# RMSNorm and SiLU over 8192 rows: loads five blocks ahead instead of four, and gamma's row on the ScalarE queue

## The chip, the cores and the metric

The kernel runs on one core of a Trainium2 chip. The metric is the device time of one execution in microseconds; smaller is better. Of the engines, it uses VectorE (DVE in the profile), ScalarE (ACT), GpSimd (POOL) and SyncE (SP). The data is moved by 16 DMA engines, which work off what SyncE, and in the changed kernel also ScalarE, issues. TensorE does nothing here.

## The reference

The input x has 8 x 1024 rows of 2048 float32 numbers; gamma has 2048 numbers, and eps is 1e-5. Each row is divided by its root mean square, multiplied by gamma and put through SiLU:

```python
rms = np.sqrt(np.mean(x ** 2, axis=-1, keepdims=True) + eps)
out = gamma * x / rms
return (out * (1 / (1 + np.exp(-out)))).astype(np.float32)
```

The input is 67 MB and so is the output. Each number is read once and written once.

## The kernel before

The 8192 rows are cut into 16 blocks (`nblk`) of 512 rows. A block is one tile of 128 partitions, and each partition holds four whole rows (`J = 4`), that is 4 x 2048 numbers or 32 KB. So a block is 4 MB, and one DMA loads it and one stores it. The tiles come from a pool of six buffers (`BUFS`), used in turn. All work on a block is done in place: the load writes the tile, VectorE and ScalarE overwrite it, and the store reads it. The buffer is free again when its store has landed.

The order of the instructions on each engine is the order in which the code is written (`manual_schedule`); the framework only adds the waits. `load(b)` (line 49) issues the load on SyncE. `stats(b)` sums the squares of the four rows: ScalarE does three of them (line 63), VectorE one (line 59), and GpSimd makes 1/rms out of the sums with a multiply-add (line 66) and a power (line 69). `finish(b)` multiplies each row by its 1/rms and by gamma on VectorE (line 74), applies SiLU on ScalarE to pairs of rows (line 78), and issues the store on SyncE (line 79).

Before the loop, gamma's row is fetched into the first partition of a tile of the same pool (line 84; it takes one of the six buffers for a while), the first `LEAD` loads are issued, and GpSimd copies gamma from that partition to all 128 (line 89) into a tile of its own. In the loop, step b does `stats(b + 1)`, then `finish(b)`, then `load(b + LEAD)`. So SyncE's queue holds, after the first loads, store 0, load 4, store 1, load 5 and so on. SyncE takes one instruction after the other: an instruction that waits holds up all those behind it.

With six buffers, of which gamma's row has the first, block k uses buffer (k + 1) mod 6. With `LEAD = 4`, load b + 4 is written where block b - 2 was, and waits for store b - 2. In the queue it stands directly behind store b.

Of the kernel before, what the change touches and what calls it, by code (L numbers as in the profile page):

```python
# [1 line left out]

# [4 lines left out]

ACT = mybir.ActivationFunctionType
ALU = mybir.AluOpType


@with_exitstack
def kernel(
    ctx: ExitStack,
    tc: tile.TileContext,
    x: bass.AP,
    gamma: bass.AP,
    eps: bass.AP,
    out: bass.AP,
):  # L20

    nc = tc.nc
    P = nc.NUM_PARTITIONS
    f32 = mybir.dt.float32
    x2 = x.flatten_outer_dims()
    o2 = out.flatten_outer_dims()
    n, d = x2.shape
    J = 4  # L30
    BUFS, LEAD = 6, 4
    nblk = n // (P * J)
    xb = x2.rearrange("(b p j) d -> b p (j d)", p=P, j=J)
    ob = o2.rearrange("(b p j) d -> b p (j d)", p=P, j=J)

    singles = ctx.enter_context(tc.tile_pool(name="singles", bufs=1))
    pool = ctx.enter_context(tc.tile_pool(name="pool", bufs=BUFS))
    small = ctx.enter_context(tc.tile_pool(name="small", bufs=4))
    psum = ctx.enter_context(tc.tile_pool(name="psum", bufs=1, space=bass.MemoryType.PSUM))

    g = singles.tile([P, d], f32)
    half = singles.tile([P, J], f32)
    junk_a = psum.tile([P, d], f32, name="junk_a")
    junk_v = psum.tile([P, d], f32, name="junk_v")
    blocks, rstds = {}, {}

    def load(b):
        xt = pool.tile([P, J * d], f32, name="xt")
        nc.sync.dma_start(out=xt, in_=xb[b])  # L49
        blocks[b] = xt  # L50

    def row(b, j):
        return blocks[b][:, j * d:(j + 1) * d]

    def stats(b):
        ss = small.tile([P, J], f32, name="ss")
        for j in range(J):
            if j == J - 1:
                nc.vector.tensor_tensor_reduce(  # L59
                    out=junk_v, in0=row(b, j), in1=row(b, j), scale=1.0, scalar=0.0,  # L60
                    op0=ALU.mult, op1=ALU.add, accum_out=ss[:, j:j + 1])
            else:
                nc.scalar.activation(out=junk_a, in_=row(b, j), func=ACT.Square,  # L63
                                     accum_out=ss[:, j:j + 1])
        var = small.tile([P, J], f32, name="var")
        nc.gpsimd.tensor_scalar(out=var, in0=ss, scalar1=1.0 / d, scalar2=float(eps),  # L66
                                op0=ALU.mult, op1=ALU.add)
        rstd = small.tile([P, J], f32, name="rstd")
        nc.gpsimd.tensor_tensor(out=rstd, in0=var, in1=half, op=ALU.pow)  # L69
        rstds[b] = rstd  # L70

    def finish(b):
        for j in range(J):
            nc.vector.scalar_tensor_tensor(out=row(b, j), in0=row(b, j), scalar=rstds[b][:, j:j + 1],  # L74
                                           in1=g, op0=ALU.mult, op1=ALU.mult)
            if j % 2:
                pair = blocks[b][:, (j - 1) * d:(j + 1) * d]
                nc.scalar.activation(out=pair, in_=pair, func=ACT.Silu)  # L78
        nc.sync.dma_start(out=ob[b], in_=blocks.pop(b))  # L79
        del rstds[b]  # L80

    with tc.manual_schedule():
        grow = pool.tile([P, J * d], f32, name="xt")
        nc.sync.dma_start(out=grow[0:1, 0:d],  # L84
                          in_=bass.AP(tensor=gamma.tensor, offset=gamma.offset, ap=[[d, 1], gamma.ap[0]]))
        for b in range(LEAD):
            load(b)
        nc.gpsimd.memset(half, -0.5)  # L88
        nc.gpsimd.partition_broadcast(g, grow[0:1, 0:d])  # L89
        stats(0)  # L90
        for b in range(nblk):
            if b + 1 < nblk:
                stats(b + 1)
            finish(b)
            if b + LEAD < nblk:
                load(b + LEAD)


# [1 line left out]
_INS = ['x', 'gamma', 'eps']  # L100
_OUTS = [((8, 1024, 2048), 'float32')]

_NUMBERS = {'eps': 9.999999747378752e-06}


# [26 lines left out]
```

## Time and profile before

| | |
|---|---|
| median of 13 runs | 322.48 us (321.2 to 323.99) |
| the profiled execution: its own time | 322.32 us |
| the profiled execution: span from first to last instruction | 320.5 us |
| VectorE busy | 181.7 us (57%) |
| ScalarE busy | 213.7 us (67%) |
| GpSimd busy | 59.5 us (19%) |
| moved by DMA | 134.24 MB, mean 419 GB/s |
| busy share of SyncE's DMA queue | 97.9% of the span of 16 DMA engines |

The span runs from the first to the last instruction of the core; the time around it (322.32 - 320.5 = 1.8 us) is launch and end. An engine's busy time counts its compute instructions. The DMA figures are means over 16 DMA engines, which means that one of them can be late without the mean showing it. Where the profile names SPq, it means SyncE's queue, in which the DMAs are issued; the time to landing runs from an issue to the moment at which all parts of the transfer have been reported.

### The profile page before, as it was taken

How to read it: one execution, taken by the hardware profiler on the slowest of the kernel's cores; microseconds unless marked ns; L12 is line 12 of the kernel's file. 1: busy time of each engine (PE TensorE's matmuls, PEld its weight loads, DVE VectorE, ACT ScalarE, POOL GpSimd, SP SyncE). 2: the span in 40 equal slices, each digit the busy share in tenths (PEclk: the TensorE clock that was granted, in tenths of full speed). 3: DMA queues.
4: the chain of work that ended last, by engine and by line, in shares of the span. 5: the costliest groups of instructions: out<-in, count | busy, mean ns of one | idle time of the engine just before them, and what ended most of it. 6: DMA issues, size and time to landing. Idle time of an engine off the chain costs nothing.

```text
span 320.5 us, 432 instructions
## 1 busy us (share of the span) xinstructions
DVE 181.7 (57%) x96; ACT 213.7 (67%) x130; POOL 59.5 (19%) x38
## 2 busy tenths in 40 slices
DVE  0209998485490934909358192762917639099500
ACT  1349999988474874748657486773857848487800
POOL 0212232213040220402104031040400404012000
DMA  8999999999999999999999999999999999997994
GB/s 316 405 442 417 433 429 413 388 446 433 425 450 409 443 438 397 458 433 414 450 417 433 450 409 450 438 413 438 425 433 446 417 438 438 425 446 331 446 429 192
DMA packets 4612, 134.24 MB, mean 419 GB/s; under 512 B 513, under 2 KB 513, under 8 KB 513
## 3 DMA queue, kind: packets, MB, share of 16 engines
q1 hardware_dynamic: 4610, 134.23, 97.9%
q14 instruction: 2, 0.02, 0.0%
HBM read 67.12 MB, written 67.11 MB: 419 GB/s over the span
## 4 chain that ended last, share of the span: by engine, by line
DMA 60%; DVE 17%; ACT 13%; issue 5%; DVEq 1%; SPq 1%; ACTq 0%
DMA xt<-in_x_dram 60%; DVE xt L74 16%; ACT xt L78 8%; ACT junk_a L63 4%; DVEq L127 1%; SPq L79 0%; DVE ss L59 0%; DVE junk_v L59 0%; SPq L49 0%; SPq L84 0%; DVEq L59 0%; ACTq L63 0%; DVEq L74 0%
## 5 line engine op out<-in xcount | busy, mean ns | idle before, releaser
L74 DVE SCALAR_TENSOR_TENSOR xt<-xt,rstd,g 128x2048 f32<-128x2048 f32 x64 | 146.1, 2346 | 1.1 <-POOL rstd L69 1.1
L63 ACT ACTIVATE junk_a<-xt 128x2048 f32<-128x2048 f32 x48 | 90.3, 1880 | 67.4 <-DMA xt<-in_x_dram 66.4
L78 ACT ACTIVATE xt<-xt 128x4096 f32<-128x4096 f32 x32 | 115.5, 3615 | 23.0 <-DVE xt L74 23.0
L59 DVE CUSTOM_DVE_ANT_0 junk_v<-xt 128x2048 f32<-128x2048 f32 x16 | 36.8, 2299 | 118.4 <-DMA xt<-in_x_dram 118.4
L66 POOL TENSOR_SCALAR var<-ss 128x4 f32<-128x4 f32 x16 | 15.0, 935 | 221.3 <-ACT junk_a L63 209.5
L69 POOL TENSOR_TENSOR rstd<-var,half 128x4 f32<-128x4 f32 x16 | 42.0, 2624 | 1.3
L63 ACT ACTIVATION_READ_ACCUMULATOR junk_a<-xt 128x1 f32 x48 | 8.9, 186 | 0.0
L89 POOL PARTITION_BROADCAST g<-xt x1 | 2.3, 2304 | 8.0 <-issue 8.0
L59 DVE DVE_READ_ACCUMULATOR2_ANT ss<- 128x1 f32 x16 | 2.3, 141 | 0.0
L63 ACT ACT_TABLE_LOAD x1 | 1.3, 1283 | 0.7 <-PEq L113 0.7
L78 ACT ACT_TABLE_LOAD x1 | 1.3, 1283 | 0.0
L88 POOL MEMSET half<- 128x4 f32 x1 | 0.1, 102 | 0.3 <-POOLq L113 0.3
L113 POOL MEMSET const-float32-0.0<- 128x1 f32 x1 | 0.1, 99 | 0.2 <-issue 0.2
L113 POOL MEMSET const-bfloat16-1.0<- 128x1 bf16 x1 | 0.1, 102 | 0.0
L113 POOL MEMSET const-uint8-127<- 128x1 uint8 x1 | 0.1, 102 | 0.0
L113 POOL MEMSET const-float32-1.0<- 128x1 f32 x1 | 0.1, 99 | 0.0
## 6 DMA issues: line engine op xcount, KB each, us to landing
xt<-in_x_dram SPq DMA_DIRECT2D x16, 4096.0 KB, 42.6
out_dram<-xt SPq DMA_DIRECT2D x16, 4096.0 KB, 33.3
xt<-in_gamma_dram SPq DMA_DIRECT2D x1, 8.0 KB
```

What stands on the lines that cost most here:

```text
L59: nc.vector.tensor_tensor_reduce(out=junk_v, in0=row(b, j), in1=row(b, j), scale=1.0, scalar=0.0, op0=ALU.mult, op1=ALU.add, accum_out=ss[ ...
L63: nc.scalar.activation(out=junk_a, in_=row(b, j), func=ACT.Square, accum_out=ss[:, j:j + 1])
L66: nc.gpsimd.tensor_scalar(out=var, in0=ss, scalar1=1.0 / d, scalar2=float(eps), op0=ALU.mult, op1=ALU.add)
L69: nc.gpsimd.tensor_tensor(out=rstd, in0=var, in1=half, op=ALU.pow)
L74: nc.vector.scalar_tensor_tensor(out=row(b, j), in0=row(b, j), scalar=rstds[b][:, j:j + 1], in1=g, op0=ALU.mult, op1=ALU.mult)
L78: nc.scalar.activation(out=pair, in_=pair, func=ACT.Silu)
L88: nc.gpsimd.memset(half, -0.5)
L89: nc.gpsimd.partition_broadcast(g, grow[0:1, 0:d])
L113: nc = _bacc.Bacc("TRN2", target_bir_lowering=False, num_devices=1)
L127: with _tile.TileContext(nc) as tc:
```

## The change

Two edits. `LEAD` goes from 4 to 5, so five loads are issued before the loop, and in the loop load b + 5 stands behind store b. The number of buffers stays at six. And gamma's row is fetched by a DMA that ScalarE issues, ahead of all its other work, instead of by the first DMA in SyncE's queue.

```diff
-    BUFS, LEAD = 6, 4
+    BUFS, LEAD = 6, 5
...
     with tc.manual_schedule():
         grow = pool.tile([P, J * d], f32, name="xt")
-        nc.sync.dma_start(out=grow[0:1, 0:d],
-                          in_=bass.AP(tensor=gamma.tensor, offset=gamma.offset, ap=[[d, 1], gamma.ap[0]]))
+        nc.scalar.dma_start(out=grow[0:1, 0:d],
+                            in_=bass.AP(tensor=gamma.tensor, offset=gamma.offset, ap=[[d, 1], gamma.ap[0]]))
         for b in range(LEAD):
             load(b)
```

With this, load b + 5 is written where block b - 1 was, and waits for store b - 1. On SyncE, 16 loads and 16 stores remain; the last five stores stand behind all loads, where there were four.

## The prediction

> **What bounds the kernel now.** I read the page's first three parts first: engines, the row of DMA digits, the queues.
>
> ```profile
> span 320.5 us, 432 instructions
> ...
> DVE 181.7 (57%) x96; ACT 213.7 (67%) x130; POOL 59.5 (19%) x38
> ...
> DMA  8999999999999999999999999999999999997994
> ...
> q1 hardware_dynamic: 4610, 134.23, 97.9%
> ```
>
> No compute engine is busy above 67%; the one DMA queue moves 134.23 MB and is busy 97.9% of the span, 9 tenths or more in nearly every slice. Only the first slice and the last four dip. So time can only come from those edges or from a change in how fast the 16 DMA engines work. A busy share is a mean over 16, so next I ask whether the queue ever runs short: SyncE's issues in order of time, and the two lines' times from issue to landing.
>
> ```profile
> 39.27 0.35 SPq L79 DMA_DIRECT2D out_dram<-xt  x1
> 39.66 0.43 SPq L49 DMA_DIRECT2D xt<-in_x_dram  x1
> ...
> 139.30 0.34 SPq L79 DMA_DIRECT2D out_dram<-xt  x1
> 139.70 0.58 SPq L49 DMA_DIRECT2D xt<-in_x_dram  x1
> ...
> 257.06 48.11 SPq L79 DMA_DIRECT2D out_dram<-xt  x4
> ```
>
> ```profile
> DMA to landing us min/median/max: 13.9/33.3/35.1
> ```
>
> That last line is of the stores (L79); the loads (L49) have:
>
> ```profile
> DMA to landing us min/median/max: 12.2/42.6/43.6
> ```
>
> Each load goes out 0.4 us behind its store and never waits. A 4.19 MB transfer needs about 9.7 us (below), so a store landing after 33.3 us found some 33.3 - 9.7 = 24 us of work queued ahead of it. The queue isn't short in the middle. The tail is where it looks short; here are windows of 1 us (the last two columns are the DMA share and GB/s):
>
> ```profile
> 293.00:294.00 1.00, 1.00 (x1) 1.00 (x1) 0.00 (x0) 1.00 0.83 360
> 294.00:295.00 1.00, 1.00 (x2) 1.00 (x1) 0.00 (x0) 1.00 0.31 131
> 295.00:296.00 1.00, 1.00 (x1) 0.76 (x1) 0.00 (x0) 1.00 0.30 131
> 296.00:297.00 1.00, 1.00 (x2) 0.33 (x1) 0.00 (x0) 1.00 1.22 524
> ```
>
> (A packet counts where it falls, so shares over 1 occur.) For two microseconds only about a third of the engines have work: store 13 is through on the others and store 14 isn't issued before ScalarE ends its Silu at 295.77 (292.15 + 3.62). It is tempting to book these 2 us as the gain of an earlier last load. So I went to the trace's landing marks, sixteen for every transfer, one per DMA engine. First and last mark: store 12 284.70 and 290.30, store 13 294.38 and 299.99, store 14 306.75 and 309.68, store 15 316.45 and 319.32. The last marks are 9.69, 9.69 and 9.64 apart, as they are over most of the run (9.69 from the median of all transfers), while the first jump by 12.37 between stores 13 and 14. The engines that idle are the ones that lead by 5.6 us; the laggards never stop, and **the laggards end the run**. Their whole path is a sum: 13.35 (last mark of load 0) + 31 x 9.69 = 313.7, + 5.6 of extra time in seven transfers = 319.3, then 1.2 to the span's end. The extras: load 1 1.06, load 3 1.00, load 4 1.06, store 3 0.34, load 7 0.63, store 5 0.80, load 12 0.70.
>
> **What the Trainium skill says.** "DMA: Bandwidth & Descriptors", Queues, rings and completion order: each DMA engine takes descriptors in order from its own ring and round-robins between queue rows at packet borders. Every engine thus runs at its own pace, as the marks show; a gamma row on the second queue need not sit behind the loads. Same page, Why a DMA increments its semaphore by 16 and not by 1: a transfer over 128 partitions uses 16 engines and is complete only when all have reported. The trace agrees: 513 packets under 512 B are 32 x 16 + 1, so gamma's is on one engine. So a load that waits for a store waits for the laggard. Same page, Issuing engines are not separate DMA queues: another issuer saves only issue time. The trace of before has nothing on ScalarE's queue.
>
> **The change, part by part.**
>
> 1. *Gamma's issue leaves SyncE.* Load 0's issue moves from 1.12 to 0.72 us, when gamma's began: 0.40. First load packets started at 2.10, so now at about 1.7 if descriptor generation doesn't collide with ScalarE's. Bounds: 0 to 0.40; I take 0.40. Gamma's 8 KB packet (0.31 us) stays on one engine in both kernels. ScalarE issues it at 0.72 and its table load (1.28 us) slips by 0.35, covered by ScalarE's wait for load 0, which lasts to 13.37. The broadcast of gamma began at 8.85, though gamma had landed at 2.5; that is 6 us of cover, and its result is first read at 26.46, against a broadcast end of 11.15: 15 us more.
>
> 2. *A fifth load up front.* Its issue is another 0.45 us on SyncE (four took 1.90), at about 2.6 us, with SyncE idle until 39.27. Store 0 now has five loads ahead of it: its slot is the sixth instead of the fifth, so it starts at about 52 instead of 42. It is issued at 39.27 either way (ScalarE sets that), 13 us early. Load 5 takes gamma's old buffer, free since 11.15, so it goes out at 39.66 unhindered.
>
> 3. *A new wait.* With six buffers, load b+5 writes where block b-1 was, so it waits for store b-1 to land on all engines; before, load b+4 waited for store b-2. In the new queue order store b-1, load b+4, store b, load b+5, store b+1, the wait ends with load b+4 and store b still queued: 2 x 9.7 = 19.4 us for the laggard, 19.4 - 5.6 = 13.8 us for a leading engine. From SyncE's issue to the first packet took 1.0 us (1.12 to 2.10), the issue itself 0.6. So the wait costs the DMA nothing. Ten loads (6 to 15) wait, each most of a 19.4 us round. Behind each on SyncE stands store b+1. It is ready early: it needs load b+2, which landed three slots (29 us) before, and the compute from a load's landing to the store ahead of it is about 15 us (load 15 lands at 280.62, store 14 goes out at 295.77). Nobody but the load into its buffer waits for that store, and it too has two transfers ahead.
>
> 4. *The tail.* Load 15 moves from slot 28 to 27, 9.7 us earlier, store 15 goes out near 304.8 - 9.7 - 0.7 = 294.4 and its turn comes at about 303.5 at the earliest engine. The leaders' idle goes: their median mark steps by 12.19 from store 13 to 14, 2.5 us too much, and ten of sixteen marks do so. Price: nothing, by the marks above, since the laggards have all 32 transfers back to back anyway. Upper bound if idle engines could pass on their share of the rate: 10 x 2.5 / 16 = 1.6 us.
>
> 5. *One turn fewer.* The queue changes from a load to a store 12 times instead of 13. Four of the thirteen loads ahead of a store (3, 4, 7, 12) took extra, 3.4 us together, 0.26 a turn. I don't know that the turn is the cause (load 1 has no store near it), so bounds are 0 and 1.06; I take 0.26.
>
> Sum: 0.40 + 0 + 0 + 0 + 0.26, so 0.7 us. The profiled execution took 322.32 with span 320.5; I expect a span of 319.8 and 321.6 for it, and from the median of 322.48, which lies 0.16 above the profiled one, **321.8 us**.
>
> **Rivals.** *The tail pays after all* (faster). If the rate is shared, so that engines with nothing to do leave bandwidth to others, the 1.6 us of part 4 come back, and with part 1 it is 322.48 - 2.0 = 320.5. For it: the dip in the windows. Against it: 32 KB packets take 1213 ns nearly always in the trace, and the laggards' 9.69 didn't shorten while the others idled. In the same case I count the extras: should most of those 5.6 us be due to stores issued close to a turn, the new order, which issues 19 us ahead, may drop 1 to 3 us of them.
>
> *Turns get dearer* (slower). The first two turns (loads 3 and 4) cost 1.0 each, later ones 0 to 0.7; the first loads had been issued in a bunch, far ahead of their turn. In the new order every store is issued some 29 us ahead of its own, and if that makes turns cost 1.0, each costs 0.74 more: two such turns eat the 0.7 gain, four put the time 2.3 us above my forecast, at 324.1; all twelve give 331. It decides against the old kernel's time plus 0.97 from about (0.7 + 0.97)/0.74 = 2.3 turns on. Against it: before, stores are 24 us ahead too, and nine turns of thirteen cost nothing.
>
> *The change does nothing*, 322.4: SyncE's early issue is lost in descriptor generation and no turn is saved. *The new wait is exposed* would need 13.8 us of delay between a landing and the next packet, against 1.6; then 10 rounds pay. *Gamma comes late* likewise: it would need to land after about 37 us for store 0 to miss its turn at 52. I give these two 0.02 together.
>
> **Numbers.** A difference of 0.3%, 0.97 us, is about what a measurement of this kernel can tell; the 13 runs spread 321.2 to 324.0. Forecast (321.8, within 0.8 of it by the unknown extras): 0.52, of which faster 0.18, same 0.33, slower 0.01. Tail or extras pay: 0.24, nearly all faster. Nothing: 0.11, of which same 0.09, slower 0.02. Dearer turns and late gamma or wait: 0.13, of which slower 0.11. Together faster 0.42, same 0.44, slower 0.14. The range leaves a tenth at each end: from the tail case, 320.2, to the dearer turns' first steps, 323.3.
>
> **What would show it.** Right: SyncE's waits list ten load waits on stores, some 18 us each; load issue to landing falls from 42.6 to about 29 us (three slots) and the store's rises from 33.3 to about 39 (four); the dip at 294 is gone, and the last microseconds have only a few engines at work for longer, 5 us, since leaders end near 313.5; the first load packets start near 1.7; the last marks still step by 9.69. Wrong: last marks stepping shorter once the leaders never idle (tail rival); more or larger extras on loads ahead of a store (dear turns); DMA digits under 9 in the middle (exposed wait); the first multiply by gamma after 26.5 us (late gamma).

## The result, and the profile after

The changed kernel takes 320.70 us (median of 11 runs, 319.77 to 321.24), the kernel before, measured beside it, 322.63 us (48 runs). The ratio is 0.9938, with a 95% interval of 0.9920 to 0.9955: 2.0 us faster. The profiled execution took 319.77 us, with a span of 318.0 us. It was the quickest of the 11, so its span shows a little more gain than the kernel has at its median.

The page's first three parts:

```profile
span 318.0 us, 433 instructions
...
DMA  8999999999999999999999999999999999999994
...
q1 hardware_dynamic: 4608, 134.22, 98.5%
```

The 7 that stood in slice 37 of the DMA row is gone, and only the first and the last slice dip. The rest looks like before, and it can't be read from this row where 2 us went. SyncE's issues in order of time (start, us, what) show the new order at work:

```profile
40.62 0.35 SPq L79 DMA_DIRECT2D out_dram<-xt  x1
41.06 0.38 SPq L49 DMA_DIRECT2D xt<-in_x_dram  x1
53.59 0.34 SPq L79 DMA_DIRECT2D out_dram<-xt  x1
64.22 0.33 SPq L49 DMA_DIRECT2D xt<-in_x_dram  x1
66.57 0.34 SPq L79 DMA_DIRECT2D out_dram<-xt  x1
83.59 0.33 SPq L49 DMA_DIRECT2D xt<-in_x_dram  x1
84.01 0.38 SPq L79 DMA_DIRECT2D out_dram<-xt  x1
...
239.68 53.21 SPq L79 DMA_DIRECT2D out_dram<-xt  x5
```

From load 6 (64.22) on, the load comes first, and from load 7 (83.59) on the store behind it follows at once: the load was held, and the store stood ready. What SyncE waited for (total us, times, longest) confirms it:

```profile
SPq L49 <- DMA out_dram<-xt: 175.6, 10, 19.0
```

Ten loads waited for stores, 17.6 us each on average. In the kernel before, no load waited. The times from issue to landing, first of the stores (L79):

```profile
DMA to landing us min/median/max: 23.6/38.3/43.0
```

and of the loads (L49):

```profile
DMA to landing us min/median/max: 12.3/29.0/51.9
```

Medians of four slots for the store and three for the load, as forecast (39 and 29). And the windows in which ten DMA engines had been idle, last columns DMA share and GB/s:

```profile
293.00:294.00 1.00, 0.00 (x0) 0.00 (x0) 0.00 (x0) 1.00 0.84 360
294.00:295.00 1.00, 0.00 (x0) 0.00 (x0) 0.00 (x0) 1.00 1.07 459
295.00:296.00 1.00, 0.00 (x0) 0.00 (x0) 0.00 (x0) 1.00 1.14 492
```

The hole is filled, and the compute engines have nothing left to do here: the tail is stores alone. At the end only the laggards, the DMA engines that lag behind the others, still have work:

```profile
313.00:314.00 1.00, 0.00 (x0) 0.00 (x0) 0.00 (x0) 1.00 0.23 98
314.00:315.00 1.00, 0.00 (x0) 0.00 (x0) 0.00 (x0) 1.00 0.15 66
```

The landing marks say the same: store 15 has its first mark at 313.51 (316.45 before) and its last at 316.77 (319.32 before). So the laggards are alone for 3.3 us, where the forecast had 5 and the kernel before 2.9. In these two profiled executions the leaders gained 2.9 us and the laggards 2.55. The laggards' path adds up as in the prediction: 12.98 (last mark of load 0, 0.37 earlier) + 31 x 9.69 + 3.4 of extras instead of 5.6 = 316.8. Of the 0.37 us that load 0 is earlier, load 1's larger extra (1.28 against 1.06) takes back more than half: load 2's last mark is at 33.66 instead of 33.82.

One thing was not forecast. These are the first instructions of GpSimd's chain and of the multiply by gamma, before:

```profile
8.85 2.30 POOL L89 PARTITION_BROADCAST g<-xt  x1 [8.03 <-issue]
...
22.95 0.19 POOL L66 TENSOR_SCALAR var<-ss 128x4 f32<-128x4 f32 x1 [11.80 <-issue]
...
26.46 9.13 DVE L74 SCALAR_TENSOR_TENSOR xt<-xt,rstd,g 128x2048 f32<-128x2048 f32 x4
```

and after:

```profile
11.03 2.30 POOL L89 PARTITION_BROADCAST g<-xt  x1 [10.21 <-issue]
...
26.43 0.19 POOL L66 TENSOR_SCALAR var<-ss 128x4 f32<-128x4 f32 x1 [13.10 <-ACT junk_a L63]
...
27.80 9.14 DVE L74 SCALAR_TENSOR_TENSOR xt<-xt,rstd,g 128x2048 f32<-128x2048 f32 x4 [1.36 <-POOL rstd L69]
```

The broadcast starts 2.2 us later, and so does what stands behind it on GpSimd: 1/rms of block 0 now comes last, and VectorE waits 1.36 us for it. (The profile puts GpSimd's wait of 13.10 down to ScalarE, whose sums of block 0 were done at 19.1; the pause before the first multiply-add was there before, 11.80, with no releaser.) Store 0 goes out at 40.62 instead of 39.27.

### The profile page after: what moved, and what is told of

Its sections match the earlier page's. It is cut to its first block, busy times and chain, and to the rows that moved or that the text cites. A ratio compares the mean times of both kernels' runs of the same rounds, so it can differ in the third digit from the quotient of the medians.

```text
span 318.0 us, 433 instructions
## 1 busy us (share of the span) xinstructions
DVE 181.9 (57%) x96; ACT 213.1 (67%) x130; POOL 58.7 (18%) x38
## 4 chain that ended last, share of the span: by engine, by line
DMA 74%; DVE 8%; ACT 6%; issue 2%; DVEq 1%; SPq 1%; POOL 0%; ACTq 0%; POOLq 0%
DMA out_dram<-xt 58%; DMA xt<-in_x_dram 16%; DVE xt L74 8%; ACT junk_a L63 3%; ACT xt L78 3%; DVEq L127 1%; SPq L49 1%; POOL rstd L69 0%; POOL var L66 0%; DVE ss L59 0%; DVEq L74 0%; ACTq L63 0%; SPq L79 0%; POOLq L66 0%
## 5 line engine op out<-in xcount | busy, mean ns | idle before, releaser
L66 POOL TENSOR_SCALAR var<-ss 128x4 f32<-128x4 f32 x16 | 18.1, 1130 | 207.7 <-ACT junk_a L63 207.7
L69 POOL TENSOR_TENSOR rstd<-var,half 128x4 f32<-128x4 f32 x16 | 38.0, 2376 | 1.3
```

## The experiments

The theory to test: the end is set by the late DMA engines, whose path is the start of load 0, 32 transfers of 9.69 us, and some extras; the fifth load saves an extra at a turn of the queue from load to store, gamma's move saves 0.4 us at the start, and the tail is worth nothing. Rivals: the tail pays; it is the new rhythm of issues that pays; what matters is that gamma's packet has a queue of its own. Each kernel ran beside the kernel before on one chip, four to a chip, and ratios are to that.

**Each edit alone.** First gamma:

```diff
-        nc.sync.dma_start(out=grow[0:1, 0:d],
+        nc.scalar.dma_start(out=grow[0:1, 0:d],
```

> Only gamma's row moves to ScalarE's queue; four loads in front stay. Start theory (part 1 of the prediction): first load packets 0.3 to 0.4 us earlier (about 1.7 us), the last landing marks step by 9.69 as before, time 322.6 - 0.4 = 322.2, ratio about 0.999. If instead gamma's packet out of SyncE's queue changed more than the start (fewer extras on the late DMA engines), the ratio would be 0.997 or less.

322.99 us, ratio 1.0020 (1.0003 to 1.0036): slower, though the first load packets did start at 1.72 us instead of 2.10. Store 0 went out at 40.23 instead of 39.27, by the delay on GpSimd shown above, while the leaders were through with load 3 at 41.6 instead of 42.1. From its issue to its first packet store 0 takes 0.8 us in the kernel with the late store below (44.48 to 45.32), and here the leaders ran dry: the packet records show two to three of the 16 DMA engines without a packet for some 0.4 us just before 41.7. By the marks, though, this cost the laggards nothing: in this profile store 0 has its last mark at 52.97 and load 4 at 63.98, where the kernel before had 54.22 and 64.97. The lead of 1 us is lost later, to extras of 4.0 us on loads 5 to 14 (1.3 before; table below). Why they are so large here, and whether they have to do with gamma's move, isn't shown. Then the lead:

```diff
-    BUFS, LEAD = 6, 4
+    BUFS, LEAD = 6, 5
```

> Only the lead goes from four to five; gamma stays on SyncE. Start theory: all of the gain but 0.4 us is here, so about 321.1, ratio 0.995. If the two edits only pay together, 322.6. The extras of the last marks over 9.69 should sum to some 3.5 us as in the changed kernel, not 5.6.

321.67 us, ratio 0.9978 (0.9966 to 0.9990): 0.7 us of gain, less than the 0.995 expected, and the profile's extras were 5.0, not 3.5. The runs also lie closer together: their standard deviation is 0.34 us, against 0.75 in the 67 runs of the kernel before beside it. The gain is at the long end of the spread. The shortest tenth of the times ends at 321.37 us (321.45 before), the longest tenth begins at 322.17 (323.35 before).

**The two together, once more.**

> The changed kernel, unaltered, beside the others on one chip. If the two edits really work together (lead alone 0.9978, gamma alone 1.002, both 0.9938), the ratio stays near 0.994 (320.4 against 322.3). If the difference between 0.9938 and the product of the two is chip and chance, it comes out at 0.996 to 0.998. Its extras on the last marks should again be lower than the 5.6 us of the kernel before: I expect 3 to 5.

321.08 us, ratio 0.9961 (0.9945 to 0.9976), extras 5.0. So the gain is 1.3 us here and was 2.0 in the first measurement; the intervals overlap, and 0.9961 lies in the range that was to mean chip and chance (0.996 to 0.998). Gamma's move, which loses 0.2% with four loads, seems to gain 0.17% with five, by the difference to the lead alone; but the two were measured on different chips and their intervals overlap. The next kernel takes gamma's own queue away and keeps the early load 0:

```diff
-    BUFS, LEAD = 6, 4
+    BUFS, LEAD = 6, 5
...
-        nc.sync.dma_start(out=grow[0:1, 0:d], ...)
         for b in range(LEAD):
             load(b)
+            if b == 0:
+                nc.sync.dma_start(out=grow[0:1, 0:d], ...)
```

> Five loads in front, and gamma's row stays on SyncE but goes out as the second DMA, behind load 0. Start theory (only the 0.4 us by which load 0 goes out earlier counts): the same as the changed kernel within 0.2 us. If it matters that gamma is on another queue (its packet out of the ring of the loads), it is slower than the changed kernel by 0.3 us or more, as the lead alone is (0.9978).

321.18 us, ratio 0.9964 (0.9947 to 0.9981), beside 0.9961 for the changed kernel on the same chip. First load packets at 1.75. So the other queue isn't needed. That load 0 going out first is what gains fits the first packets, but this kernel's interval overlaps that of the lead alone (0.9978), so the times don't show it. In this kernel gamma comes later still, store 0 goes out at 43.16, and with five loads in front that costs nothing.

**The tail.** Load 15 one step earlier, nothing else:

```diff
-            if b + LEAD < nblk:
+            if b + LEAD < nblk and b + LEAD not in blocks and b + LEAD not in done:
                 load(b + LEAD)
+            if b + LEAD == nblk - 2:
+                load(nblk - 1)
+                done.add(nblk - 1)
```

> The kernel before, but load 15 is issued one step earlier, right behind load 14, so that five stores follow the last load as in the changed kernel, and store 13 to 14 leaves no DMA engine idle. The forecast's part 4 says it pays nothing: ratio 1.000 within 0.002, 322.3. The tail rival says 1.6 us: 0.995, 320.7.

322.13 us, ratio 0.9999 (0.9986 to 1.0013). The same windows of this kernel:

```profile
294.00:295.00 1.00, 0.00 (x0) 1.00 (x1) 0.00 (x0) 1.00 1.14 492
295.00:296.00 1.00, 0.00 (x0) 1.00 (x1) 0.00 (x0) 1.00 1.06 459
```

The hole that is so plain in the profile of before (0.31 and 0.30 here) is filled, the leaders end at 313.76 instead of 316.45, and the time is the same, within 0.14%. The 1.6 us of the tail rival, 0.5%, are excluded: this idle time of the leaders costs nothing.

**The rhythm.** Two ways to issue stores away from the turn while the order of transfers stays the old one. Five buffers, so that a load waits for the store two places before it:

```diff
-    BUFS, LEAD = 6, 4
+    BUFS, LEAD = 5, 4
```

> Lead four as before, but five buffers, so a load waits for the store of two places before it in the queue, as in the changed kernel, and the next store is issued right behind it; order of transfers as before. Rhythm theory (extras come where stores are issued close to the moment at which the queue turns from a load to a store; with the new wait they are issued half a round away from it): extras in the middle of the run go from about 1.3 us to about 0, time 322.6 - 1.3 = 321.3, ratio 0.996. Turn-count theory (one turn fewer is what pays, and the early turns are the dear ones): the order is the old one, so 322.6, ratio 1.000.

321.91 us, ratio 0.9989 (0.9975 to 1.0002), with 135.6 us of load waits on stores. And stores that come late because there is more to compute:

```diff
+        if 4 < b < 13:    # in stats(b), on VectorE
+            for k in range(2):
+                nc.vector.tensor_tensor_reduce(out=junk_v, in0=row(b, k), in1=row(b, k), ...)
...
+            if j == 3 and 4 <= b < 12:    # in finish(b), on ScalarE
+                for k in range(2):
+                    nc.scalar.activation(out=junk_a, in_=row(b, 3), func=ACT.Square)
```

> The kernel before, with two added sums of squares on VectorE (results unused) and two added Squares on ScalarE ahead of a block's last Silu, for blocks 4 to 12 and 4 to 11: stores 4 to 11 are issued some 9 us later, half a round away from the turn from a load to a store, with the DMA queue still 14 us deep. The output is the same. Rhythm theory: extras in the middle vanish as in the changed kernel, about 321.3, ratio 0.996. Turn-count theory: 322.6, ratio 1.000. Should the queue run short for the leading engines, nothing is lost as long as the late ones have work: still 322.6 or less.

321.93 us, ratio 0.9980 (0.9962 to 0.9998). Neither reaches 0.996, and the late issue gains as much as the lead alone on the same chip (0.9978). So the rhythm isn't worth the 1.3 us of its theory; that it has a part of 0.1 or 0.2% can't be excluded by these runs. The five-buffer kernel also shows that the new wait as such costs nothing.

**The front.** Five loads in front, none after store 0, then a lead of four:

```diff
-        for b in range(LEAD):
+        for b in range(LEAD + 1):
...
-            if b + LEAD < nblk:
+            if b and b + LEAD < nblk:
```

> Gamma on SyncE as before; five loads in front, none after store 0, and from then on a lead of four: only the front of the queue is that of the changed kernel, and stores 0 and 1 stand next to each other. Front theory (the gain of the lead is made in the first 70 us, where two dear turns become one and store 0 no longer goes out just as it is needed): as the lead alone, 0.998, about 321.6. If the gain comes from the wait's rhythm or from the tail: 1.000, 322.3.

321.78 us, ratio 0.9988 (0.9975 to 1.0001): between the two values expected, so it doesn't decide alone. The extras of the last marks over 9.69 us, one profile per kernel, say more. They are worked out from the trace; load 1, which has 0.2 to 1.3 in every kernel with no store near it, is left out, and so is 0.46 on load 2 in gamma second:

```
                          load 3  load 4  later loads  stores
four in front
  before                    1.00    1.06     1.3        1.1
  five buffers              1.00    1.46     0.6        1.0
  late issue                1.34    1.07     1.1        1.0
  tail only                 0.91    1.43     0.4        1.1
  gamma only                0.13    1.32     4.0        0
five in front
  changed kernel            0       1.47     0          0.8
  changed kernel again      0       1.36     1.9        0.8
  lead only                 0       1.48     2.0        0.6
  gamma second              0       1.69     2.1        0.2
  front only                0       1.51     1.7        0.9
```

With store 0 queued in time behind load 3, load 3 has an extra of 0.9 to 1.3. It has none where a fifth load stands behind it, and 0.13 where store 0 came a little late (gamma only). Load 4 has an extra in every row, and a store stands behind it in every row. In the profile of a lead of six (below), where the first store stands behind load 5, loads 3 and 4 have none and load 5 has 1.50: the extra follows the turn. So an early turn costs 0.9 to 1.7 us, and the lead has one of them where the old kernel has two: 2.3 on the mean of the first four rows, 1.5 in the lower five. That is 0.8 us, about what the lead alone gains (0.7).

But the agreement is not a proof. What the later turns cost varies from 0 to 2.1 us from one profile to the next, and with five in front it isn't less: later loads and stores have 1.5 to 2.4 us together in the first four rows and 2.3 to 2.7 in the last four, which takes most of the 0.8 us back. The bookkeeping leaves nothing out, since in every profile the time of the execution is the last mark plus 3.0 us. And 0.8 us saved every time would show in the shortest times, too. In the three kernels with five loads in front and gamma first on SyncE (lead alone, front only, and the one with a late store below) the shortest tenth of the times is only 0.1 us below that of the kernel before, the longest tenth 0.8 to 1.4: what the lead takes away there is the long times. (The changed kernel, with the early start, gained 1.2 and 0.5 us in the shortest tenth of its two measurements, which have only 11 and 10 times.) No execution of the kernel before of 323 us or more was profiled; the one profile of such a length with four in front and no added work, gamma only (323.07), has its time in the extras of later loads. So that the saved turn is what gains 0.7 us isn't shown, and why the first profile of the changed kernel, its quickest run, had no later extras stays open.

**A late first store**, with four and with five in front. The same edit in both:

```diff
+            if b == 0 and j == 3:
+                for k in range(3):
+                    nc.scalar.activation(out=junk_a, in_=row(b, 3), func=ACT.Square)
```

> The kernel before with three Squares more on ScalarE (results unused) ahead of block 0's last Silu: store 0 goes out about 6 us later, near 45.5. Front theory: with four loads in front, the leading DMA engines are through with load 3 at 42.1 and the last at 44.4, so the cover of store 0 (39.3 + 1.0 to its first packet) is 1.8 us for the leaders and 4 us for the laggards; they idle 4 us and 2 us, the run is longer by about 2 us, 324.2, ratio 1.006. If the front had slack enough, 1.000.

326.18 us, ratio 1.0134 (1.0094 to 1.0174). Store 0 went out at 44.48, and the DMA engines stood still, all of them, here in windows of 2 us:

```profile
40.00:42.00 2.00, 2.00 (x2) 1.97 (x2) 0.00 (x0) 1.00 0.69 295
42.00:44.00 2.00, 2.00 (x2) 2.00 (x1) 0.00 (x0) 1.00 0.00 0
44.00:46.00 2.00, 2.00 (x2) 2.00 (x2) 0.00 (x0) 1.00 0.62 262
```

The price was twice what I expected. One reason is in the marks: load 3, with no store behind it in time, had no extra, and load 1 had 0.6 less than before. So load 3's last mark came at 42.9 and not at 44.4, and the laggards had little more cover than the others. Store 0's last mark was 3.94 us late, and the runs are longer by 4.3 by the ratio (four runs; 3.8 between the medians). With five in front:

> The same late store 0 with a lead of five (gamma on SyncE). Front theory: store 0's turn comes at 52 at the earliest, so 45.5 + 1.0 is still in time: no DMA engine idles, and the time is that of the lead alone, ratio 0.998. If the late store costs here too, about 1.004, the fifth load is not what covers it.

321.76 us, ratio 0.9977 (0.9963 to 0.9991), the same as the lead alone. The windows:

```profile
40.00:42.00 2.00, 2.00 (x2) 1.97 (x2) 0.00 (x0) 1.00 1.22 524
42.00:44.00 2.00, 2.00 (x2) 2.00 (x1) 0.00 (x0) 1.00 0.68 295
44.00:46.00 2.00, 2.00 (x2) 2.00 (x2) 0.00 (x0) 1.00 1.14 492
```

No hole. (A packet of 32 KB counts where it falls, so a single window can be low.) This is what the fifth load buys for certain: store 0 may be 5 us late for nothing.

**Fewer turns.** The changed kernel with loads in pairs:

```diff
-            if b + LEAD < nblk:
-                load(b + LEAD)
+            for q in (b + LEAD - 1, b + LEAD):
+                if b % 2 and q < nblk:
+                    load(q)
```

> The changed kernel with its loop's loads issued in pairs after every second block: two stores, two loads, two stores and so on, so that the queue turns from a load to a store 7 times instead of 12, with the same buffers. Turn theory (an extra of 0.26 us or more per turn): five turns fewer take 1.3 us, 319.8 against 322.1, ratio 0.992. If turns are not the cause: as the changed kernel, 0.996. Should the pairs let the queue run short, slower.

320.65 us, ratio 0.9942 (0.9921 to 0.9963). Its extras are 1.36 on load 4, 0.72 on later loads and 0.9 on stores. It may be better than the changed kernel (0.9961 and 0.9938 in its two measurements), but the intervals overlap, and the interval ends just short of the 0.992 that five turns at 0.26 would give. Not settled.

**A lead of six**, with six buffers, to see the new wait where nothing covers it:

```diff
-    BUFS, LEAD = 6, 5
+    BUFS, LEAD = 6, 6
```

> The changed kernel with a lead of six and six buffers: load b + 6 waits for store b, which stands right ahead of it, and store b + 1 stands behind. Now nothing is queued when the wait ends, so the wait is exposed: from the last mark of a store to the first packet of the next load some 1.4 us in each of ten rounds, and the leaders wait for the laggards besides. 320.7 + 14 to 20 us, 335 to 341. If the DMA keeps busy anyway, 321.

355.36 us, ratio 1.102 (1.097 to 1.107).

```profile
SPq L49 <- DMA out_dram<-xt: 234.2, 10, 34.5
```

As in the changed kernel ten loads wait, but here the queue is empty when the wait ends, and the DMA row shows it in its eights and sevens:

```profile
DMA  8999999969899799798897988989989899999996
```

The mechanism is the expected one and the price isn't: loads 6 to 15 have extras of 3.5 to 3.8 us each, where I had reckoned 1.4. A load's time from issue to landing was 13.3 us at the median, with nothing ahead of it: 3.6 more than the 9.69 of a transfer in a full queue. Ten times 3.6 is 36 us, close to the loss of 34.7 against the changed kernel.

## Why the prediction was right, and where it was off

The time lay in the range and the kernel is faster, as forecast; but by 0.6%, where I had held it slightly likelier that it stays within 0.3%. The size was short: 0.7 us forecast, 2.0 measured at first (interval 1.5 to 2.6) and 1.3 in the repetition (0.8 to 1.8). That the range took in 320.70 owes something to luck: its lower end, 320.2, came from the tail rival, which is refuted.

1. *Gamma's issue leaves SyncE*: 0.40 forecast; 0.37 by the first packets (2.10 to 1.73) and by load 0's last mark (13.35 to 12.98). Right in size for the start, though load 1's extra left only 0.16 of it at load 2's last mark in that profile. The experiment with gamma second (0.9964 beside 0.9961) shows that gamma's own queue isn't needed for it. This agrees with the Trainium skill, "DMA: Bandwidth & Descriptors", Issuing engines are not separate DMA queues, by which issuing from another engine saves only the time of the issue. Wrong in its cover. I counted 15 us until the gamma tile is read, and overlooked who stands behind the broadcast on GpSimd: block 0's 1/rms, ready at 23.23 + 1.06 = 24.3 for a multiply at 26.46, 2.2 us of cover. GpSimd came 3.5 us later, and the first multiply by gamma at 27.80, after the 26.5 that the prediction had named as a sign of being wrong. "ScalarE sets that", of store 0's 39.27, fell with it: 40.62. In the changed kernel the fifth load hides it. Alone, the edit measured 0.2% slower, which no rival of mine had; its cause is open, since the laggards were ahead until load 4.

2. *A fifth load up front*: hidden, as said. That the deeper front makes a later store harmless I priced at nothing. For a store 0 that is 5 us late it decides (1.0134 with four in front, 0.9977 with five); whether the 1.35 us of the changed kernel would have cost anything without it isn't shown.

3. *The new wait costs nothing*: right. Ten waits of 17.6 us, no slice under 9, medians to landing as forecast. The rival that has it exposed needed a thin queue, and a lead of six has one and shows it, at 3.6 us a round and not the 1.6 that I had put together from issue and first packet.

4. *The tail is worth nothing*: right, and shown by the experiment that changes only the tail (0.9999). The tail rival is refuted: the leaders end 2.7 us earlier there for no gain.

5. *One turn fewer*: this is the term that was mis-sized. I took the mean over thirteen turns, 0.26, with 1.06 as the upper bound. What the fifth load gains beside the start measured 0.7 (the lead alone, 0.3 to 1.1). The turn that is saved is an early one, and in the profiles these cost 0.9 to 1.7 each where the store stood behind the load in time; the net is 0.8. The sizes match, but the later extras of the same profiles take most of the 0.8 back, and the gain is at the long end of the spread and hardly at the short one. So the turn is a candidate, and the cause of the 0.7 stays open. The two measured terms, 0.40 + 0.7 = 1.1, come close to the repetition (1.3). The first measurement's other 0.7 us stays unexplained: its profile, of the quickest run, lacks the later extras that the repetition has.

The slower rival, dearer turns, is not what happened, but later loads with five in front did cost 1.7 to 2.1 us in four of five profiles against 0.4 to 1.3 in the four undisturbed ones with four in front. It was nearer than I thought. Its sum was also wrong: one dearer turn at 0.74, not two, eats the 0.7 us of gain, and four are 3.0 us above the forecast (2.3 above the old kernel), which makes 324.8 and not 324.1.

## What to carry to other kernels

Where a kernel is bound by DMA, look at when each of the sixteen engines reports, not at their mean share: idle time of those that lead was worth nothing here, however plain the hole in the profile. What a first transfer that goes out 0.4 us earlier gains has to be followed beyond it: more than half was gone two loads later in one profile here. Load as far ahead as leaves other transfers queued at the moment at which a load's wait for a store ends: two of them were enough, none cost 10%, and one was not tried. Look at the whole spread of the times before a gain in the median is put down to a step that every execution has. When an instruction is moved, follow also what stands behind its reader on that engine: the cover is as long as that of the tightest among them.

## What the runs showed of the hardware

- The 16 DMA engines don't keep pace. A 32 KB packet took 1213 ns in nine of ten cases, but four to six engines fell behind at single moments, mostly on the last packets of a load with a store behind it (in the kernel before from 60.0 us on, with load 4 through at 62.0 on the first engine), and did not catch up while the others had work: 5.6 us between first and last mark of store 13 in the kernel before, 3.3 in the changed one. Which they are, and why these, was not tried.
- Some extras on stores fall together with the packets of queue 14, which the profile marks as instruction: 8 KB each, at 108.09 and 148.03 us in the kernel before, within the slots of stores 3 and 5 (0.34 and 0.80 us). That one causes the other was not tried, and with gamma only two such packets, at 107.64 and 147.60, go with no extra.
- GpSimd's broadcast began at 8.8 to 9.6 us in the eight kernels that fetch gamma first on SyncE, and at 10.6 to 11.2 in the five with gamma on ScalarE, though gamma's packet was through within 2.4 us in both the kernel before and the changed one. With gamma second, where gamma landed at 13.16, it began at 13.29. What GpSimd does in that pause, and in the 11.8 us after the broadcast, no run tells.
